# A bilinear matmul kernel: row tiles loaded and transposed three at a time, one product of the first triple moved to the front, and the opening loads put in another order

## The chip, the cores and the metric

The kernel runs on one core of a Trainium2 chip. A core has five engines that run side by side: TensorE (PE, with its weight loads shown as PEld), VectorE (DVE), ScalarE (ACT), GpSimd (POOL) and SyncE (SP). DMAs are issued from the queues of SP, ACT and POOL. The metric is device microseconds of one execution; lower is better.

## The reference

```python
"x":  (16, 512, 1024) float32,  "w1", "w2": (1024, 768) float32

def reference(x, w1, w2):
    y1 = np.matmul(x, w1)
    y2 = np.matmul(x, w2)
    return (np.tanh(y1) * y2).astype(np.float32)
```

## The kernel before, in words

The 8192 rows of x are 64 row tiles of 128 rows (`MT`). Both weights together have 1536 columns, which the kernel takes as three blocks of 512: `a` (the first 512 columns of w1), `g` (the last 256 of w1 and of w2 together) and `b` (the first 512 of w2). The inner dimension of 1024 is cut into two halves of four 128-row slices (`KH` = 4). All operands of the matmuls are float16.

The first four row tiles (`HEAD`) are multiplied plainly: 8 matmuls for each block, in the order a, g, b, while the weights are still arriving (`plain`, `mm`, L421 of the kernel before). The other 60 tiles form 20 triples. A triple's 18 block products (3 row tiles x 2 halves x 3 blocks) are replaced by 15 products p0 to p14 of four matmuls each (`product`, L444). Their left operands are a row tile's transposed half or a sum of such halves (`A_SUMS`, made on VectorE at L412, named S10, S3, S15 and so on); the right operands are weight blocks or sums of blocks (`B_SUMS`, made once on VectorE at L403, written B24, B26 and so on). Between the products, results are copied out of PSUM on ScalarE (copies and seeds, L448) and added on VectorE (L454); `C_OPS` lists these steps with what each needs. Names such as p7.0 mean product p7 of triple 0. Outputs are a tanh on ScalarE (L457) and a multiplication on VectorE (L462): m0, m1 and m2 for the three 512-column parts of a triple, mh0 to mh2 for the 256-column parts. In the first four triples m0 to m2 are done as two halves of 256 columns (`HALVED`).

**Who decides the order.** `Planner` is a list scheduler that runs when the kernel is built. Each step is an `op` with a cost, a due time, what it needs, and for DMAs a time at which it should land (`lands`, `LANDING`). The order that it finds for each engine is then pinned; on the chip each engine works in that order, with semaphore waits. TensorE's order of products is written by hand: `PE_ORDER` for a triple in general, `FIRST_ORDER` for triple 0, `LAST_ORDER` for the last. An entry with a plus belongs to the triple before.

**Loads of the start.** ACT's queue loads a0 to a3. SP's queue loads the halves of the first four row tiles (x00 is half 0 of tile 0), a4 to a7 and the g slices, as float32 into the `arena` or into `early_x` (`on_sp`, L338, L345, L348). VectorE and ScalarE cast them to float16 (L359 on VectorE, L357 on ScalarE). POOL's queue loads the b slices and whole row tiles, cast by the DMA itself (L350, L353): first a `gate` that reads the cast slice g0 (L484), then the eight b slices, then row tiles 6, 4, 5, then tiles 7, 8, 9. Tiles 0 to 6 are transposed on TensorE (`transpose_pe`, L371: four 128x128 transposes for a half tile, named PT60 for half 0 of tile 6) and evacuated (e60).

**Loads and transposes later.** Tiles 7 to 63 are transposed by a DMA on SP's queue (T7 to T63, L378), out of 8 float16 buffers (`xh`) into 12 transposed ones (`xt`). From tile 10 on, a load (L10 and so on) on POOL's queue stands behind a hold: POOL copies one column of the transpose of four tiles earlier (`AHEAD` = 4, `hold_loads`, L481), so POOL stops until that transpose has landed, and then issues one load. SP's queue also carries the output stores (L418). ScalarE sums the absolute values of every tile (L381, D7 and so on), for a check at the end.

**Set aside already.** For tiles 0 to 2 the b product is copied out of its bank by ScalarE (yb0, L431) and multiplied much later on VectorE (L435).

Of the kernel before, what the change touches and what calls it, by code (L numbers as in the profile page):

```python
# [226 lines left out]
def kernel(  # L227
# [68 lines left out]
    def xh_place(mt):  # L296
        return (mt - HEAD) % XH_BUFS

    def xh_before(mt):
        return next((m for m in range(mt - 1, 1, -1) if xh_place(m) == xh_place(mt)), None)  # L300

# [18 lines left out]
    def xh(mt):  # L320
        return xh_bufs[xh_place(mt)]
# [11 lines left out]
    def fill(e, chain):  # L333
        for cols in FILL:
            constants(bank(chain), cols)

    def load_first(e, mt, h):
        pin(nc.sync.dma_start(x_first[mt][:, half(h)], xf[mt][:, half(h)]))  # L338

    def cast_x(e, mt, h):  # L340
        copy(e, xh(mt)[:, half(h)], x_first[mt][:, half(h)])

# [8 lines left out]

    def load_x(e, mt):
        pin(nc.gpsimd.dma_start(xh(mt), xf[mt]))  # L353

# [82 lines left out]
    def place(i, name):  # L437
        if name[0] == "c":
            return bank((i, name))
        return c_bufs[name, i % C_BUFS]  # L440

    def product(e, i, dst, a, b, begins):
        for k in range(KH):
            pin(nc.tensor.matmul(place(i, dst), x_operand(i, a)[:, k, :], w_rhs(b, k),  # L444
                                 start=begins and k == 0, stop=k == KH - 1, skip_group_check=True))
# [36 lines left out]

    def gate(e, s, k):
        pin(nc.gpsimd.tensor_copy(held, w_cols(s, k)[:, :1]))  # L484

# [3 lines left out]
    FINE = (5, 36, 37, 45)  # L489
    START = 28.6  # L490
    ORIGIN = START - 6 * SLOT

# [16 lines left out]
    rows_in = (HEAD + 2, HEAD, HEAD + 1)  # L509
    GATE = ("g", 0)  # L510
    in_order = on_sp[4:] + late + [f"x{mt}" for mt in rows_in]
# [3 lines left out]
    for n in in_order:  # L515
        now += 1.25 if n in in_order[-3:] else size[n[0]]
        lands[n] = now + (LAG if now > LAG_FROM else 0.0)
# [3 lines left out]
    for n, what in enumerate(on_sp):  # L521
        before = [f"L{on_sp[n - 1]}"] if n else []
        if what[0] == "x":
            op(f"L{what}", {"sp": 0.05}, 0.1 * n - 100, [], load_first, int(what[1]), int(what[2]), issued=before, lands=lands[what])
        else:
            s, k = what[0], int(what[1])
            j = slices.index((s, k))
            old = [slices[i - SLOTS] for i in range(j, j + 1 + (s == "g")) if i >= SLOTS]
            op(f"L{what}", {"sp": 0.05}, 0.1 * n - 100, [], load_w, s, k, int(what[2]) if s == "g" else None, issued=before,
               behind=[f"c{a}{b}" for a, b in old], lands=lands[what])  # L530
    op("gate", {"pool": 0.1}, 0.0, ["c%s%d" % GATE], gate, *GATE)
    for n, what in enumerate(late):
        op(f"c{what}", {"pool": 0.58}, 0.1 * n, [], load_w, "b", int(what[1]), issued=[f"c{late[n - 1]}" if n else "gate"], lands=lands[what])
    for n, mt in enumerate(rows_in):
        op(f"L{mt}", {"pool": 0.58}, 1 + 0.1 * n, [], load_x, mt, issued=[f"L{rows_in[n - 1]}" if n else f"c{late[-1]}"],
           behind=[f"cx{m}{h}" for m in range(2, HEAD) for h in range(2) if xh_place(m) == xh_place(mt)], lands=lands[f"x{mt}"])
# [7 lines left out]
    all_casts = [f"c{s}{k}" for s, k in slices if s != "b"]  # L544
    for t in range(2):
# [12 lines left out]
    for mt in range(HEAD):  # L558
# [4 lines left out]
        op(f"D{mt}", {"act": 1.05}, START + 8, [f"Lx{mt}0", f"Lx{mt}1"], abs_x, mt, hold=11 + 4 * mt)  # L563
    for mt in rows_in:
        for h in range(2):
            by_pe(mt, h, lands[f"x{mt}"] - 2, f"L{mt}")

# [16 lines left out]
    def reuse_out(mt):  # L584
        return [f"st{mt - O_BUFS}"] if mt >= HEAD + O_BUFS else []

# [80 lines left out]
    for i in range(TRIPLES):  # L667
# [10 lines left out]
        for o in C_OPS:  # L678
# [10 lines left out]
            if kind in ("seed", "copy", "add"):  # L689
                before = []  # L690
                if o[3][0] == "s":
                    before = [f"{r}.{i - C_BUFS}" for r in readers[o[3]]] if i >= C_BUFS else all_casts
                if kind == "add":
# [7 lines left out]
            if kind in ("t", "th"):  # L701
                lo, n = (0, F) if kind == "t" else (F, G)
                op(f"{name}.{i}", {"act": 0.5 if n == F else 0.285}, due, needs, c_tanh, i, r, o[4], lo, n, o[5],
                   behind=reuse_out(mt) + ([f"{FIRST_READER[name]}.{i}"] if i == TRIPLES - 1 and name in FIRST_READER else []), chains=chains)
            elif kind == "m" and i < HALVED:
                for t in range(2):
# [6 lines left out]
    for mt in range(MT):  # L713
        i = (mt - HEAD) // 3 if mt >= HEAD else -1
        if mt < HEAD:
            kept = mt == HEAD - 1
            for t in range(2 if mt < 2 else 0):
                op(f"st{mt}{'ag'[t]}", {"sp": 0.05}, 1e3, outs[mt][t:t + 1], store, mt, t * F, (F, G)[t], behind=[f"p12.{11 + 2 * mt}"], xfer=0.5)
            if mt >= 2:
# [9 lines left out]
        else:  # L729
            op(f"st{mt}", {"sp": 0.05}, slot_of[max(i, 0), "p2"] + 12, outs[mt], store, mt, behind=late, xfer=1.0)  # L730
    for mt in range(BY_PE, MT):
        back = xh_before(mt)
        free = [] if back is None else ([f"PT{back}0", f"PT{back}1"] if back < BY_PE else [f"T{back}"]) + ([f"D{back}"] if back >= HEAD else [])
        before = f"L{mt - 1}" if mt > BY_PE else f"L{rows_in[-1]}"
# [4 lines left out]
        op(f"T{mt}", {"sp": 0.05}, None, [f"L{mt}"], transpose, mt, issued=[f"T{mt - 1}"] if mt > BY_PE else [],  # L739
           behind=xt_readers[mt - XT_BUFS] if mt >= XT_BUFS and mt - XT_BUFS != HEAD - 1 else [], xfer=1.2, latency=LANDING.get(mt, 1.0 if mt < HEAD + 6 else 3.0))  # L740
    for mt in range(HEAD, MT):
        i, r = divmod(mt - HEAD, 3)
        soon = START + 6 + 1.1 * r if i == 0 else slot_of[i, "p7"] + (2, 0, -4, -8)[min(i, 4) - 1] + 4.3 * r
        op(f"D{mt}", {"act": 1.05}, soon + 4, [f"L{mt}"], abs_x, mt, hold=soon)

# [123 lines left out]
```

## Time and profile before

| | |
|---|---|
| median of 3 runs | 297.87 us (297.68 to 299.07) |
| profiled execution: its own time | 297.88 us |
| profiled execution: span in the profile | 296.3 us |
| mean granted TensorE clock | 0.997 |
| PE, DVE, ACT, POOL busy | 289.6, 257.4, 226.3, 49.2 us |
| DMA traffic | 63.51 MB, mean 214 GB/s |

The span is what the profile covers; the device time adds what lies around it, 1.6 us here. "Idle before" in a row is the engine's idle time just ahead of those instructions, with what ended it. A matmul's start is recorded, its end is modelled, so that the records of successive matmuls overlap.

### The profile page before, as it was taken

Reading aid. Unit: us, or ns where it says so; the run is one execution under the profiler, and the core shown is the slowest. Engines: PE = TensorE matmul, PEld = TensorE weight load, DVE = VectorE, ACT = ScalarE, POOL = GpSimd, SP = SyncE. Lnnn points to the kernel's source line nnn. Section 1 sums busy time; section 2 is a strip of 40 time slices with the busy share of each in tenths; the row PEclk is TensorE's granted clock in tenths of the full one; section 3 lists DMA queues with packets and bytes.
Section 4 is the critical chain, followed back from the end, with each engine's and each line's share of the span. In section 5 each row is a group of like instructions: output and inputs, shape, how many; then the busy total and the mean of one; then the engine's idle time right before and its main releaser. Section 6 shows DMA issues by size and latency. Waiting matters only on the chain. (4 is left out here: it accounts for less than half of the span.)

```text
span 296.3 us, 4677 instructions
## 1 busy us (share of the span) xinstructions
PE 289.6 (98%) x1374; PEld 131.9 (45%) x1374; DVE 257.4 (87%) x552; ACT 226.3 (76%) x453; POOL 49.2 (17%) x129
## 2 busy tenths in 40 slices
PE   7999999999999999999999999999999999999994
PEld 3344444444444444444444444444444444444442
DVE  1679899989999998888989898898989989898785
ACT  3586899699978979797797988768686776868442
POOL 0063033020213021102110120031012110000000
PEclk9999999999999999999999999999999999999998
DMA  6999999999999999999999999999999999340334
GB/s 215 388 307 204 183 160 149 229 197 237 224 253 271 215 198 252 237 144 253 233 234 162 221 191 218 195 310 223 221 235 232 261 269 298 127 162 25 136 141 164
DMA packets 84715, 63.51 MB, mean 214 GB/s; under 512 B 62800, under 2 KB 66896, under 8 KB 84688
## 3 DMA queue, kind: packets, MB, share of 16 engines
q1 hardware_dynamic: 73888, 44.84, 62.9%
q0 software_dynamic: 9792, 16.78, 37.2%
q10 hardware_dynamic: 1008, 1.57, 1.5%
q8 instruction: 11, 0.18, 0.3%
q14 instruction: 16, 0.13, 0.2%
HBM read 39.85 MB, written 25.17 MB: 219 GB/s over the span
## 5 line engine op out<-in xcount | busy, mean ns | idle before, releaser
L444 PE MATMUL bank<-b,early_x 128*128 128x512 f16 x640 | 148.3, 379 | 0.1
L444 PEld LDWEIGHTS <-early_x 128*128 128x128 f16 x800 | 78.1, 98 | 95.0 <-issue 0.7
L454 DVE TENSOR_TENSOR bank<-bank,arena 128x512 f32<-128x512 f32 x100 | 69.6, 697 | 14.4 <-ACT arena L448 8.8
L448 ACT ACTIVATE arena<-bank 128x512 f32<-128x512 f32 x100 | 59.4, 596 | 28.7 <-PE bank L444 28.5
L462 DVE TENSOR_TENSOR o<-o,bank 128x256 f32<-128x256 f32 (+1 forms) x132 | 64.3, 512 | 6.1 <-ACT o L457 5.4
L381 ACT ACTIVATE junk<-xh 128x1024 f16<-128x1024 f16 x60 | 63.3, 1054 | 0.2
L444 PEld LDWEIGHTS <-xT 128*128 128x128 f16 x400 | 39.0, 98 | 46.6 <-issue 0.3
L444 PE MATMUL bank<-b,xT 128*128 128x512 f16 x240 | 58.3, 379 | 0.0
L457 ACT ACTIVATE o<-bank 128x256 f32<-128x256 f32 (+1 forms) x80 | 34.5, 436 | 16.0 <-DVE bank L454 11.7
L444 PE MATMUL bank<-wh,xT 128*128 128x512 f16 x160 | 41.1, 379 | 0.0
L444 PE MATMUL bank<-wh,early_x 128*128 128x512 f16 x160 | 40.9, 379 | 0.0
L481 POOL CAST held<-xT 128x1 f32<-128x1 f16 x54 | 12.3, 227 | 159.4 <-DMA xT<-xh 159.3
L353 POOL DMA_DIRECT2D xh<-in_x_dram x60 | 31.9, 532 | 17.2 <-issue 7.7
L412 DVE TENSOR_TENSOR early_x<-early_x,xT 128x512 f16<-128x512 f16 x80 | 33.2, 419 | 0.5
L448 ACT ACTIVATE bank<-bank 128x512 f32<-128x512 f32 x40 | 21.5, 574 | 7.3 <-DVE bank L454 6.2
L457 ACT ACTIVATE o<-arena 128x512 f32<-128x512 f32 x40 | 25.1, 628 | 1.2 <-DVE arena L454 1.2
L421 PE MATMUL bank<-wh,xT 128*128 128x512 f16 x72 | 18.5, 379 | 0.5 <-DVE wh L359 0.3
L412 DVE TENSOR_TENSOR early_x<-xT,xT 128x512 f16<-128x512 f16 x40 | 16.8, 419 | 0.0
L412 DVE TENSOR_TENSOR early_x<-xT,early_x 128x512 f16<-128x512 f16 x40 | 16.8, 419 | 0.0
L454 DVE TENSOR_TENSOR bank<-arena,bank 128x512 f32<-128x512 f32 x20 | 13.9, 695 | 2.4 <-ACT o L457 0.9
L454 DVE TENSOR_TENSOR arena<-bank,arena 128x512 f32<-128x512 f32 x20 | 13.7, 683 | 0.2
L454 DVE TENSOR_TENSOR arena<-arena,bank 128x512 f32<-128x512 f32 x20 | 13.6, 681 | 0.0
(47 smaller groups left out, 134.7 us busy)
## 6 DMA issues: line engine op xcount, KB each, us to landing
out_dram<-o SPq DMA_DIRECT2D x58, 384.0 KB, 5.3
xh<-in_x_dram POOLq DMA_DIRECT2D x60, 256.0 KB, 6.8
arena<-in_w_dram SPq DMA_DIRECT2D x12, 256.0 KB, 5.6
early_x<-in_x_dram SPq DMA_DIRECT2D x8, 256.0 KB, 5.0
arena<-in_w_dram ACTq DMA_DIRECT2D x4, 256.0 KB, 5.9
wh<-in_w_dram POOLq DMA_DIRECT2D x8, 128.0 KB, 5.1
out_dram<-o SPq DMA_DIRECT2D x4, 256.0 KB, 6.5
xT<-xh SPq DMA_TRANSPOSE x57, 6.9
```

The source lines that it names most:

```text
L353: pin(nc.gpsimd.dma_start(xh(mt), xf[mt]))
L381: pin(nc.scalar.activation(junk[:, :src.shape[-1]], src, ACT.Abs, scale=scale, accum_out=sums[:, column:column + 1]))
L412: pin(engine[e].tensor_tensor(x_operand(i, v), x_operand(i, a), x_operand(i, b), OP[how]))
L421: pin(nc.tensor.matmul(bank(chain)[:, :rhs.shape[-1]], xt(mt)[:, k, :], rhs, start=first, stop=k == KO - 1, skip_group_check=True))
L444: pin(nc.tensor.matmul(place(i, dst), x_operand(i, a)[:, k, :], w_rhs(b, k), start=begins and k == 0, stop=k == KH - 1, skip_group_check=T ...
L448: pin(nc.scalar.activation(place(i, dst), place(i, src), ACT.Copy, scale=float(sign)))
L454: pin(nc.vector.tensor_tensor(place(i, dst), a, b, ALU.add if signs == (1, 1) else ALU.subtract))
L457: pin(nc.scalar.activation(out_tile(HEAD + 3 * i + r)[:, lo:lo + n], place(i, src)[:, :n], ACT.Tanh, scale=float(sign)))
L462: pin(nc.vector.tensor_tensor(o, o, place(i, src)[:, at:at + n], ALU.mult))
L481: pin(nc.gpsimd.tensor_copy(held, xt(mt)[:, 0, :1]))
```

## The change

It has five parts.

1. **p7.0 early.** p7 of triple 0 leaves the fixed sequence of products and is planned at 13.0 us, among the plain a products. It needs the first half of row tile 6, which SP's queue now loads as float32 (x60, behind x01 and ahead of x11) into a free part of the arena, and VectorE casts. The slots of the arena change places (s376 behind s64), and a slot's first use waits only for the casts of what was staged in it, so that the copy of p7.0 can be written early.
2. **FIRST_ORDER** of triple 0 becomes 10 6 1 12 9 11 14 8.
3. **POOL's loads of the start** are mixed: b0, b4, b1, b5, the second half of tile 6, tile 4, b2, the two halves of tile 5, b6, b3, b7. Row tile 5's and 6's halves are transfers of their own.
4. **Batches of a triple.** From tile 10 on there is one hold for three loads, on the second transpose of the triple before. Within a triple the loads go in the order second, first, third. The tiles of the first triple are taken in the order 6, 4, 5, those of the second 7, 9, 8. Landing times for the planner are written out for tiles 7 to 15.
5. **m0.0 and m2.0 set aside.** Both banks are copied on ScalarE into out tiles of triple 2 that are not yet in use (of tiles 11 and 10), and the multiplications are done whole on VectorE, not before 55 and 54 us. Row tile 0 is stored in one DMA instead of two.

The numbers of matmuls, transposes, row loads' bytes and stores' bytes are unchanged. The core of the diff (helpers that only rename or pass on an argument are left out):

```diff
-FIRST_ORDER = "7 10 1 6 12 9 11 14 8"
+FIRST_ORDER = "10 6 1 12 9 11 14 8"
...
-    AHEAD, FREE = 4, 3
-    LANDING = {HEAD + 6: 5.8, HEAD + 7: 4.1, HEAD + 8: 3.9}
+    FREE = 3
+    TURNS = (2, 0, 1), (0, 2, 1)
+    LANDING = {7: 35.9, 9: 37.2, 8: 38.4, 10: 44.9, 11: 46.1, 12: 47.3, 13: 53.8, 14: 55.0, 15: 56.2}
+    rows = list(range(HEAD)) + [HEAD + 3 * i + r for i in range(TRIPLES) for r in (TURNS[i] if i < len(TURNS) else (0, 1, 2))]
+    turn = {mt: n for n, mt in enumerate(rows)}
...
+    ASIDE = {"m0": (HEAD + 7, 55.0), "m2": (HEAD + 6, 54.0)}
...
+    S_NAMES.insert(1, S_NAMES.pop(0))
...
+    STAGED = SLOTS - 2
...
+    def slot_casts(name):
+        n = S_NAMES.index(name) * C_BUFS
+        return [f"c{s}{k}" for j, (s, k) in enumerate(slices) if s != "b" and n <= j % SLOTS < n + C_BUFS] + [f"cx{HEAD + 2}0"] * (n <= STAGED < n + C_BUFS)
...
+    def c_aside(e, r, src, borrowed):
+        pin(nc.scalar.copy(out_tile(borrowed)[:, :F], place(0, src)))
+
+    def aside_mul(e, r, borrowed):
+        o = out_tile(HEAD + r)[:, :F]
+        pin(nc.vector.tensor_tensor(o, o, out_tile(borrowed)[:, :F], ALU.mult))
...
+    P7 = 13.0
...
+    position["p7", 0] = 0
...
-    plan.strict = [f"{p}.{i}" for _, i, p in sequence]
+    plan.strict = [f"{p}.{i}" for _, i, p in sequence if (p, i) != ("p7", 0)]
+    slot_of[0, "p7"] = P7
...
-    on_sp = "x00 x10 x20 x30 x01 x11 a4 a5 x21 a6 x31 a7".split() + [f"g{k}{t}" for k in range(KH) for t in range(2)]
-    late = [f"b{k}" for s, k in slices if s == "b"]
-    rows_in = (HEAD + 2, HEAD, HEAD + 1)
+    on_sp = "x00 x10 x20 x30 x01 x60 x11 a4 a5 x21 a6 x31 a7".split() + [f"g{k}{t}" for k in range(KH) for t in range(2)]
+    by_pool = "b0 b4 b1 b5 x61 x4 b2 x51 x50 b6 b3 b7".split()
+    GATES = {"b0": ("cg0", w_cols("g", 0)[:, :1])}
...
-    for mt in range(BY_PE, MT):
+    loads = rows[BY_PE:BY_PE + FREE] + [rows[n + r] for n in range(BY_PE + FREE, MT, 3) for r in (1, 0, 2)]
+    for n, mt in enumerate(loads):
...
-        if mt >= BY_PE + FREE:
-            op(f"H{mt}", {"pool": 0.1}, None, [f"T{max(mt - AHEAD, BY_PE)}"], hold_loads, max(mt - AHEAD, BY_PE), issued=[before])
+        if n >= FREE and n % 3 == 0:
+            held_by = rows[BY_PE + n - 2]
+            op(f"H{mt}", {"pool": 0.1}, None, [f"T{held_by}"], hold_loads, held_by, issued=[before])
```

More of the change, by code (lines that the diff above doesn't have):

```diff
@@ L296, in xh_place @@
     def xh_place(mt):
-        return (mt - HEAD) % XH_BUFS
+        return (turn[mt] - HEAD) % XH_BUFS
     def xh_before(mt):
-        return next((m for m in range(mt - 1, 1, -1) if xh_place(m) == xh_place(mt)), None)
+        return next((m for m in rows[turn[mt] - 1:1:-1] if xh_place(m) == xh_place(mt)), None)
     pin = tc.keep_in_program_order
@@ L335, in fill, with x_staged @@
             constants(bank(chain), cols)
+    def x_staged(mt, h):
+        return x_first[mt][:, half(h)] if mt < HEAD else arena[:, STAGED * F:(STAGED + 1) * F]
     def load_first(e, mt, h):
-        pin(nc.sync.dma_start(x_first[mt][:, half(h)], xf[mt][:, half(h)]))
+        pin(nc.sync.dma_start(x_staged(mt, h), xf[mt][:, half(h)]))
     def cast_x(e, mt, h):
-        copy(e, xh(mt)[:, half(h)], x_first[mt][:, half(h)])
+        copy(e, xh(mt)[:, half(h)], x_staged(mt, h))
     def load_w(e, s, k, t=None):
@@ L350, in load_w, with load_x @@
             pin(nc.gpsimd.dma_start(w_cols(s, k), wr[1][:, k, :F]))
-    def load_x(e, mt):
-        pin(nc.gpsimd.dma_start(xh(mt), xf[mt]))
+    def load_x(e, mt, cols=slice(0, K)):
+        pin(nc.gpsimd.dma_start(xh(mt)[:, cols], xf[mt][:, cols]))
     def copy(e, dst, src):
@@ L481, in hold_loads, with gate @@
         pin(nc.gpsimd.tensor_copy(held, xt(mt)[:, 0, :1]))
-    def gate(e, s, k):
-        pin(nc.gpsimd.tensor_copy(held, w_cols(s, k)[:, :1]))
+    def gate(e, src):
+        pin(nc.gpsimd.tensor_copy(held, src))
     MM = 0.2158
@@ L514 @@
     now = 9.2
-    for n in in_order:
-        now += 1.25 if n in in_order[-3:] else size[n[0]]
+    for n in arrivals:
+        now += 1.25 if n in by_pool and n[0] == "x" and len(n) == 2 else size[n[0]]
         lands[n] = now + (LAG if now > LAG_FROM else 0.0)
@@ L527 @@
             j = slices.index((s, k))
-            old = [slices[i - SLOTS] for i in range(j, j + 1 + (s == "g")) if i >= SLOTS]
+            js = range(j, j + 1 + (s == "g"))
+            old = [f"c{a}{b}" for a, b in (slices[i - SLOTS] for i in js if i >= SLOTS)] + [f"cx{HEAD + 2}0"] * (STAGED in js)
             op(f"L{what}", {"sp": 0.05}, 0.1 * n - 100, [], load_w, s, k, int(what[2]) if s == "g" else None, issued=before,
[L530 to L536, printed above, removed]
+               behind=old, lands=lands[what])
+    op(f"cx{HEAD + 2}0", {"dve": 0.37}, lands["x60"] - 1, ["Lx60"], cast_x, HEAD + 2, 0,
+       behind=[f"cx{m}{h}" for m in range(2, HEAD) for h in range(2) if xh_place(m) == xh_place(HEAD + 2)])
+    issued, x_loads = [], {(HEAD + 2, 0): (f"cx{HEAD + 2}0", lands["x60"])}
+    for n, what in enumerate(by_pool):
+        if what in GATES:
+            after, src = GATES[what]
+            op(f"gate{what}", {"pool": 0.1}, 0.1 * n, [after], gate, src, issued=issued)
+            issued = [f"gate{what}"]
+        if what[0] == "b":
+            name = f"c{what}"
+            op(name, {"pool": 0.58}, 0.1 * n, [], load_w, "b", int(what[1]), issued=issued, lands=lands[what])
+        else:
+            mt, h = int(what[1]), what[2:]
+            free = [f"cx{m}{k}" for m in range(2, HEAD) for k in range(2) if xh_place(m) == xh_place(mt)]
+            name = f"L{mt}{'abc'[int(h)] if h else ''}"
+            op(name, {"pool": 0.58}, 0.1 * n, [], load_x, mt, half(int(h)) if h else slice(0, K), issued=issued, behind=free, lands=lands[what])
+            for k in range(2):
+                if h in ("", str(k)):
+                    x_loads[mt, k] = name, lands[what]
+        issued = [name]
+    last_early = name
     landed = {}
@@ L543 @@
             op(f"c{s}{k}", CAST.get(f"{s}{k}", CAST[s]), landed[s, k] + 0.3, [f"L{n}" for n in loads], cast_w, s, k)
-    all_casts = [f"c{s}{k}" for s, k in slices if s != "b"]
     for t in range(2):
@@ L563 @@
         op(f"D{mt}", {"act": 1.05}, START + 8, [f"Lx{mt}0", f"Lx{mt}1"], abs_x, mt, hold=11 + 4 * mt)
-    for mt in rows_in:
+    for mt in rows[HEAD:BY_PE]:
         for h in range(2):
-            by_pe(mt, h, lands[f"x{mt}"] - 2, f"L{mt}")
+            by_pe(mt, h, x_loads[mt, h][1] - 2 - 0.1 * h * (mt == HEAD + 1), x_loads[mt, h][0])
     def made(mt):
@@ L584, in reuse_out @@
     def reuse_out(mt):
-        return [f"st{mt - O_BUFS}"] if mt >= HEAD + O_BUFS else []
+        aside = [f"{name}.0" for name, (borrowed, _) in ASIDE.items() if mt == borrowed]
+        return aside + [f"st{mt - O_BUFS}"] if mt >= HEAD + O_BUFS else []
     def finals(mt, s, due, last):
@@ L691 @@
                 if o[3][0] == "s":
-                    before = [f"{r}.{i - C_BUFS}" for r in readers[o[3]]] if i >= C_BUFS else all_casts
+                    before = [f"{r}.{i - C_BUFS}" for r in readers[o[3]]] if i >= C_BUFS else slot_casts(o[3])
                 if kind == "add":
@@ L704 @@
                    behind=reuse_out(mt) + ([f"{FIRST_READER[name]}.{i}"] if i == TRIPLES - 1 and name in FIRST_READER else []), chains=chains)
+            elif i == 0 and name in ASIDE:
+                borrowed, at = ASIDE[name]
+                op(f"y{name}.0", {"act": 0.5}, due + 1, [n for n in needs if n[0] != "t"], c_aside, r, o[4], borrowed, chains=chains)
+                op(f"{name}.0", {"dve": 0.6}, at + 6, [f"y{name}.0"] + [n for n in needs if n[0] == "t"], aside_mul, r, borrowed, hold=at)
+                outs[mt].insert(0, f"{name}.0")
             elif kind == "m" and i < HALVED:
```

19 lines of the change are left out of this document (10 added, 9 removed).

## The prediction

> **What bounds the kernel now.** I read the page first, then TensorE's timeline, because a busy share of a pipelined engine hides short gaps.
>
> ```profile
> PE 289.6 (98%) x1374; PEld 131.9 (45%) x1374; DVE 257.4 (87%) x552; ACT 226.3 (76%) x453; POOL 49.2 (17%) x129
> ...
> L444 PE MATMUL bank<-b,early_x 128*128 128x512 f16 x640 | 148.3, 379 | 0.1
> ```
>
> TensorE is busy in 98% of the span, and the largest group of product matmuls had 0.1 us of idle time ahead of its 640 instructions: once the triples run, nothing makes it wait. But a matmul's end is modelled (379 ns each), so I count from start to start in the timeline (columns: start, duration, engine and line, tiles, how many):
>
> ```profile
> 12.37 1.03 PE L421 MATMUL bank<-wh,xT 128*128 128x512 f16 x4
> 13.52 0.40 PE L371 MATMUL bank<-ident_h,xh 128*128 128x128 f16 x4
> 14.19 1.02 PE L421 MATMUL bank<-wh,xT 128*128 128x512 f16 x4 [0.27 <-DVE wh L359]
> 15.05 0.39 PE L371 MATMUL bank<-ident_h,xh 128*128 128x128 f16 x4
> 15.27 1.11 PE L421 MATMUL bank<-wh,xT 128*128 128x512 f16 x4
> 16.22 1.03 PE L421 MATMUL bank<-wh,xT_kept 128*128 128x512 f16 x4
> 17.15 1.24 PE L421 MATMUL bank<-wh,xT 128*128 128x512 f16 x5
> ...
> 24.09 4.91 PE L421 MATMUL bank<-wh,xT 128*128 128x512 f16 x22
> 28.84 0.61 PE L371 MATMUL bank<-ident_h,xh 128*128 128x128 f16 x8
> 29.29 0.59 PE L421 MATMUL bank<-wh,xT 128*128 128x512 f16 x2
> ...
> 32.34 4.92 PE L444 MATMUL bank<-b,early_x 128*128 128x512 f16 x20
> 37.13 1.02 PE L444 MATMUL bank<-wh,early_x 128*128 128x512 f16 x4
> ```
>
> From 24.09 to 28.84 are 22 matmuls: 0.216 us each, so a product of four is 0.864. From 28.84 to 29.29 two half tiles are transposed: 0.22 each. What is over is lost time. While the a slices arrive: 13.52 - 12.37 - 0.864 = 0.29; 14.19 - 13.52 - 0.22 = 0.45; 0.09 ahead of 16.22; 0.07 ahead of 17.15; together 0.90. In the first triple: 37.13 - 32.34 - 20 x 0.216 = 0.47. These 1.37 us are all that the change can win in the stretch that it rearranges; the order of the last triple isn't touched. The sum below is made against 297.88, the profiled execution's own time, of which 1.6 lie outside its span of 296.3; the median of the three runs is 297.87. Of that, 1.37 is 0.46%, and about 0.5%, 1.5 us, is what a measurement of this kernel can tell from no change.
>
> **The change part by part.** *p7 of triple 0 among the a products.* p7.0 (0.864, today behind the transposes of 28.84) and the transpose of its half tile (0.22, one of that block) move to about 12.7. The half tile x60 is now loaded on SP's queue ahead of x11, a4 and all that follows. What one more piece costs there is told by VectorE's casts, each of which waited for a landing:
>
> ```profile
> 10.73 0.43 DVE L359 CAST xh<-early_x 128x512 f16<-128x512 f32 x1 [0.18 <-DMA early_x<-in_x_dram]
> 11.41 0.43 DVE L359 CAST wh<-arena 128x512 f16<-128x512 f32 x1 [0.25 <-DMA arena<-in_w_dram]
> 12.08 0.43 DVE L359 CAST wh<-arena 128x512 f16<-128x512 f32 x1 [0.24 <-DMA arena<-in_w_dram]
> ```
>
> These are x11, a4 and a5: a piece every 0.68. x60 takes x11's place at 10.73, so that with cast, transpose and evacuation p7.0 can start near 12.5. All behind it lands 0.68 later: TensorE reaches the first g product at 17.15 + 0.68 = 17.83, but with 0.864 + 0.22 = 1.08 of later work done. Won: 1.08 - 0.68 = 0.40. The lower end is -0.28, if x60 itself comes a piece late and p7.0, fixed in its place, holds up what stands behind it; the upper is the whole 0.90. I take 0.40, the queue being paced by its data in row after row. The added cast of 0.43 lies in VectorE's waits between these casts, 0.18 to 0.25 each, and so delays one of them by some 0.2 before the next landing absorbs it; without them each cast behind would be 0.43 late.
>
> *First triple, and the b slices mixed with row tiles.* The products of triple 0 now begin with p10, half tiles are transposed between b products, and b6, b3, b7 come last. From the first g product to the first that needs b7 TensorE has 57 matmuls and five half tiles: 57 x 0.216 + 5 x 0.22 = 13.4, so it gets there at 31.2. When does b7 land? Today's POOL queue stops once for a landing, ahead of the third row tile, and two queries of single issues give the landings of the eighth slice and of that tile:
>
> ```profile
> 24.03 1.06 POOL L353 DMA_DIRECT2D xh<-in_x_dram  x2 [1.05 <-DMA wh<-in_w_dram]
> ```
>
> ```profile
> L350 POOL DMA_DIRECT2D wh<-in_w_dram x1: 587/587/587, 21.3 to 21.3; - x1
> ...
> DMA to landing us min/median/max: 5.5/5.5/5.5
> ```
>
> ```profile
> L353 POOL DMA_DIRECT2D xh<-in_x_dram x1: 535/535/535, 24.0 to 24.0; - x1
> ...
> DMA to landing us min/median/max: 6.6/6.6/6.6
> ```
>
> The slice lands at 26.8 and three tiles later it is 30.6: 1.27 a tile. The change takes half a tile out of POOL's queue and puts it into SP's, so b7, now behind all of them, lands at about 30.7: 0.5 ahead of TensorE. VectorE then makes two sums for p12:
>
> ```profile
> 29.89 1.29 DVE L403 TENSOR_TENSOR b<-b,b 128x1024 f16<-128x1024 f16 x2
> ```
>
> With 1.3 for them and 0.4 for a row sum between, p12's operand is there at 32.4, and TensorE, with p6 and p1 (1.73) and b7's first product ahead of it, comes at 33.2. Row tiles in earlier mean that the sums behind the lost 0.47 start earlier too. I take 0.30 of it. Ends: +0.47, and -0.8 if b7 comes a tile later (31.97 against 31.2).
>
> The Trainium skill, "DMA: Bandwidth & Descriptors", section "Anatomy of one DMA — SWDGE (gpsimd) path", speaks against cutting tiles up: it fits about 2.0 us as fixed cost of each DMA. Paid in line, POOL's one additional transfer would put b7 at 32.7 and this sum 1.5 higher. The rows disagree: whole tiles follow each other at 1.27, so no fixed 2.0 is paid in line.
>
> *m0.0 and m2.0 set aside.* Four half-bank multiplications leave VectorE between 42 and 45 us, two whole-bank ones come back after 55, and ScalarE gets two copies out of banks. A piece of ScalarE's timeline, and two windows (behind the span: TensorE, weight loads, VectorE, ScalarE):
>
> ```profile
> 42.09 0.60 ACT L457 ACTIVATE o<-bank 128x512 f32<-128x512 f32 x1 [0.15 <-DVE bank L454]
> 42.58 1.05 ACT L381 ACTIVATE junk<-xh 128x1024 f16<-128x1024 f16 x1
> ```
>
> ```profile
> 40.00:50.00 10.00, 10.00 (x48) 4.54 (x47) 9.97 (x24) 9.76 (x20) 2.31 (x5) 1.00 1.20 177
> 50.00:60.00 10.00, 10.00 (x48) 4.43 (x46) 9.95 (x26) 7.24 (x15) 1.58 (x6) 1.00 1.10 205
> ```
>
> VectorE, full from 40 to 50 (9.97), gets room. ScalarE takes on 2 x 0.60 with 0.24 free, which pushes an Abs sum into the next window, where 2.76 are free; without that cover a copy or seed stands behind an Abs sum and TensorE waits up to 1.05, once. TensorE waits for neither engine there today, so there is nothing to win: 0, with that lower end.
>
> *Loads and transposes by triples.* POOL's holds fall from 54 to 18, and each lets three loads go. Of the DMA in the window from 38 to 44 us:
>
> ```profile
> q0 software_dynamic: 525, 0.98, 98.0%
> q1 hardware_dynamic: 8, 0.00, 0.2%
> ...
> xT<-xh SPq DMA_TRANSPOSE x2, 6.5
> ```
>
> Two transposes (q1) were issued in it, and none moved data while the row loads (q0) ran: the memory side works in turns. So a round counts, from hold to hold in POOL's timeline; the slowest of the early ones:
>
> ```profile
> 59.95 0.18 POOL L481 CAST held<-xT 128x1 f32<-128x1 f16 x1 [5.61 <-DMA xT<-xh]
> ...
> 74.09 0.19 POOL L481 CAST held<-xT 128x1 f32<-128x1 f16 x1 [4.57 <-DMA xT<-xh]
> ```
>
> 14.1 us for four tiles with their stores (these are the holds that read the transposes four tiles apart): 3.5 a tile, so 10.6 for three. TensorE's triple lasts 15 x 0.864 = 12.96, and the batch gains on it. Cost 0. Its start is VectorE's first sum of triple 1:
>
> ```profile
> 36.28 0.43 DVE L412 TENSOR_TENSOR early_x<-xT 128x512 f16<-128x512 f16 x1 [0.63 <-DMA xT<-xh]
> ```
>
> The bytes ahead of T7 are the same, so it lands near 36.3 as today, and VectorE again idles there while TensorE, fed by sums already made, doesn't. Stores on SP now stand behind three transposes at a time; the next writer of their out tile is three triples off, which covers it.
>
> Sum: 297.88 - 0.40 - 0.30 = 297.2 us.
>
> **The rivals.** *Nothing is won*: the idle time only moves, because TensorE is bound by landings until 17 us and b7's margin of 0.5 is used up: 297.9. Against it: 1.08 of work leaves a stretch without idle time. *b7 late*: POOL's queue, with one transfer more, stops again as at 24.03 and b7 comes a tile later: 0.8 paid, the 0.30 not won, 298.3. The page's fixed 2.0 would make it 298.7 by the same mechanism. *T7 late*: VectorE works in order, and behind its first sum of triple 1 stand the adds of triple 0. Up to about 0.5 is covered; from there each microsecond is one of TensorE, so that T7 two tiles (2.5) late gives 297.2 + 2.0 = 299.2, and 2.9 late 299.6. For it: three transposes are now issued together; against: the same three stand first in SP's queue today. *The round, slower than before*: held on a transpose of its predecessor, a triple's round takes longer than TensorE's 12.96. That is the point from which it decides. If three tiles took 13.5, nearly as long as four do today, TensorE would lose 0.54 in each of some 16 triples, less a lead of about 3 from the start: +5.8, 303. The turns seen above speak against it, since a turn of three loads is shorter than one of four. *Faster by over 1.5*: the whole 1.37 and something else besides; nothing shows that.
>
> **How the numbers follow.** The forecast has 0.50, nothing won 0.22, b7 late 0.10, T7 late 0.08 (half of it past 1.5 us), the round 0.07, faster by over 0.5% 0.03. Slower by over 0.5%: 0.04 + 0.07, and 0.05 for two of the smaller delays together, taken from the first three: 0.16. Within 0.5%: the remaining 0.81. The range goes from 296.6, nearly all of the 1.37 won, to 299.6, T7 2.9 late; it leaves out the round and the far ends.
>
> **What would show it.** Right: the first g product near 17.8; triple 0 from p6 on without lost time over 0.1; p14.0, today at 37.13, near 36.3, and the distance kept to the end; holds 9 to 12 apart until buffers, not transposes, pace them. Wrong: TensorE waiting for a wh landing near 31, VectorE idle over 1 us at a sum that reads xT, or lost time that returns once in a triple. A time under 296.4 would mean idle time that I haven't seen.

## The result, and the profile after

The changed kernel takes 311.6 us (median of 6 runs, 310.09 to 313.01) against 297.81 for the kernel before (6 runs): the ratio is 1.0453, 95% interval 1.0417 to 1.0489. It is slower by 13.8 us; the forecast was 297.2. The profiled execution took 310.09 us, 308.5 of them in the span. Some executions of any kernel here are disturbed and some per cent longer; the times below leave them out, and from the profiles of e6 and e10, which are of such executions, only the places of waits are read.

The opening went as forecast. TensorE's timeline after:

```profile
12.85 1.03 PE L457 MATMUL bank<-wh,xT 128*128 128x512 f16 x4
...
17.63 1.24 PE L430 MATMUL bank<-wh,xT 128*128 128x512 f16 x5
...
31.34 2.75 PE L457 MATMUL bank<-b,early_x 128*128 128x512 f16 x12
33.93 0.59 PE L430 MATMUL bank<-wh,xT 128*128 128x512 f16 x2
34.36 1.89 PE L457 MATMUL bank<-b,early_x 128*128 128x512 f16 x8
36.12 1.02 PE L457 MATMUL bank<-wh,early_x 128*128 128x512 f16 x4
```

p7.0 runs at 12.85, the first g product starts at 17.63, and from p6 at 31.34 to p14 at 36.12 there are 22 matmuls in 4.78 us, 0.217 each: no lost time. p14.0 is 1.01 us earlier than before (37.13).

What was lost is in the page's groups. Behind the busy times come TensorE and VectorE, then ScalarE's tanhs that read a sum in the arena and write a row tile's output (two in a triple, t2 for its third row tile and t1 for its second), then POOL's holds:

```profile
PE 292.6 (95%) x1374; PEld 131.8 (43%) x1374; DVE 254.3 (82%) x552; ACT 222.5 (72%) x454; POOL 42.3 (14%) x94
...
L457 PE MATMUL bank<-b,early_x 128*128 128x512 f16 x640 | 149.0, 379 | 6.7 <-ACT arena L461 6.7
...
L467 DVE TENSOR_TENSOR bank<-bank,arena 128x512 f32<-128x512 f32 x100 | 69.3, 693 | 30.2 <-ACT arena L461 29.2
...
L470 ACT ACTIVATE o<-arena 128x512 f32<-128x512 f32 x40 | 24.6, 626 | 23.5 <-DMA out_dram<-o 19.4
...
L501 POOL CAST held<-xT 128x1 f32<-128x1 f16 x18 | 4.5, 249 | 196.4 <-DMA xT<-xh 196.4
```

and t2 in the kernel before:

```profile
L457 ACT ACTIVATE o<-arena 128x512 f32<-128x512 f32 x40 | 25.1, 628 | 1.2 <-DVE arena L454 1.2
```

Read from the right: ahead of these tanhs ScalarE stood idle 23.5 us instead of 1.2, and 19.4 of them ended with an *output store* (DMA out_dram<-o). An out tile is used again nine row tiles later, so t2 of triple 10 writes where row tile 27, of triple 7, still lay. Behind t2, in ScalarE's order, stand the copies and seeds; VectorE waits 29.2 us for these, TensorE 6.7 and more. One such stall, in the timeline of all engines (SP's rows are issues):

```profile
150.38 0.83 SPq L427 DMA_DIRECT2D out_dram<-o  x1
...
158.11 2.64 SPq L387 DMA_TRANSPOSE xT<-xh  x2
...
160.85 0.53 SPq L427 DMA_DIRECT2D out_dram<-o  x1
161.47 1.30 SPq L387 DMA_TRANSPOSE xT<-xh  x1
...
163.73 1.15 ACT L470 ACTIVATE o<-arena 128x512 f32<-128x512 f32 x2 [1.94 <-DMA out_dram<-o]
164.78 1.06 ACT L461 ACTIVATE bank<-bank 128x512 f32<-128x512 f32 x2
165.41 1.02 PE L457 MATMUL bank<-wh,early_x 128*128 128x512 f16 x4 [0.81 <-ACT bank L461]
```

From 151.2 to 158.11 SP's queue stands still: its head is the transpose of row tile 37, whose load hasn't landed. Behind two transposes stands the store of row tile 27, issued at 160.85. t2 starts at 163.73, having waited 1.94, then the seeds, and TensorE has waited 0.81. From triple 10 to triple 18 each of the nine t2 starts 0.08 us behind the landing of such a store; counted by these landings the waits are 21.1 us (the page puts 1.7 of them down to VectorE).

How long SP's queue stood at a transpose whose load hadn't landed (total, times, longest), after and before:

```profile
SPq L387 <- DMA xh<-in_x_dram: 141.8, 19, 15.8
```

```profile
SPq L378 <- DMA xh<-in_x_dram: 71.0, 28, 16.0
```

The store's place in SP's order is not what is new. In the kernel before the first store of triple 7 also stands behind transposes of triple 11, but it is issued at 148.41, and the t2 that needs it runs at 161.27. There the transposes are early: from triple 5 on a triple's first transpose lands 8.5 to 18.9 us ahead of the first row sum that reads it. I call that distance the lead; after the change it is 0.5 to 3.0 us in triples 3 to 10.

Why is the load late? POOL's timeline and, for the same round (the way from one hold to the next), SP's:

```profile
176.16 0.18 POOL L501 CAST held<-xT 128x1 f32<-128x1 f16 x1 [11.26 <-DMA xT<-xh]
176.70 1.59 POOL L362 DMA_DIRECT2D xh<-in_x_dram  x3 [0.35 <-issue]
190.28 0.18 POOL L501 CAST held<-xT 128x1 f32<-128x1 f16 x1 [11.99 <-DMA xT<-xh]
```

```profile
183.79 4.89 SPq L387 DMA_TRANSPOSE xT<-xh  x3
```

A round is a chain in which no second batch of loads is under way: 0.54 from hold to loads, 7.09 until the first transpose can be issued, 6.49 until the second has landed and the next hold runs. This round takes 14.1 us, while TensorE's triple takes 12.95.

### The profile page after: what moved, and what is told of

Same layout as the page of the kernel before. It is cut to its first block, busy times and chain, and to the rows that moved or that the text cites. A ratio compares the mean times of both kernels' runs of the same rounds, so it can differ in the third digit from the quotient of the medians.

```text
span 308.5 us, 4589 instructions
## 1 busy us (share of the span) xinstructions
PE 292.6 (95%) x1374; PEld 131.8 (43%) x1374; DVE 254.3 (82%) x552; ACT 222.5 (72%) x454; POOL 42.3 (14%) x94
## 5 line engine op out<-in xcount | busy, mean ns | idle before, releaser
L467 DVE TENSOR_TENSOR bank<-bank,arena 128x512 f32<-128x512 f32 x100 | 69.3, 693 | 30.2 <-ACT arena L461 29.2
L461 ACT ACTIVATE arena<-bank 128x512 f32<-128x512 f32 x100 | 57.7, 596 | 12.8 <-PE bank L457 12.8
L475 DVE TENSOR_TENSOR o<-o,bank 128x256 f32<-128x256 f32 (+1 forms) x128 | 62.1, 512 | 5.4 <-ACT o L470 4.4
L457 PEld LDWEIGHTS <-xT 128*128 128x128 f16 x400 | 38.3, 98 | 50.1 <-issue 5.6
L470 ACT ACTIVATE o<-bank 128x256 f32<-128x256 f32 (+1 forms) x80 | 33.5, 438 | 27.4 <-DVE bank L467 26.5
L457 PE MATMUL bank<-wh,xT 128*128 128x512 f16 x160 | 41.0, 378 | 1.2 <-ACT o L470 1.1
L470 ACT ACTIVATE o<-arena 128x512 f32<-128x512 f32 x40 | 24.6, 626 | 23.5 <-DMA out_dram<-o 19.4
L501 POOL CAST held<-xT 128x1 f32<-128x1 f16 x18 | 4.5, 249 | 196.4 <-DMA xT<-xh 196.4
L430 PE MATMUL bank<-wh,xT 128*128 128x512 f16 x72 | 19.5, 379 | 0.1
L467 DVE TENSOR_TENSOR bank<-arena,bank 128x512 f32<-128x512 f32 x20 | 13.8, 688 | 0.3 <-PE bank L457 0.3
L390 ACT ACTIVATE junk<-wh 128x768 f16<-128x768 f16 x16 | 13.6, 848 | 0.0
```

The source lines that it names most:

```text
L390: pin(nc.scalar.activation(junk[:, :src.shape[-1]], src, ACT.Abs, scale=scale, accum_out=sums[:, column:column + 1]))
L430: pin(nc.tensor.matmul(bank(chain)[:, :rhs.shape[-1]], xt(mt)[:, k, :], rhs, start=first, stop=k == KO - 1, skip_group_check=True))
L461: pin(nc.scalar.activation(place(i, dst), place(i, src), ACT.Copy, scale=float(sign)))
L467: pin(nc.vector.tensor_tensor(place(i, dst), a, b, ALU.add if signs == (1, 1) else ALU.subtract))
L470: pin(nc.scalar.activation(out_tile(HEAD + 3 * i + r)[:, lo:lo + n], place(i, src)[:, :n], ACT.Tanh, scale=float(sign)))
L501: pin(nc.gpsimd.tensor_copy(held, xt(mt)[:, 0, :1]))
```

## The experiments

Theory A was the round itself, B the stores' place in SP's order, C another part of the change. Each kernel is the changed one with the edit shown, but for e2, which is the kernel before. "TensorE's last product" is the last row of its timeline, 291.13 before and 303.28 after; a profile shows in it what TensorE lost in that one execution. A row of the holds gives the first and the last start and their count; from these comes the mean round, 13.21 us after (18 holds from 37.1 to 261.7). The planner makes the order on SP anew for each kernel. Beside the edits shown, e1, e6 and e10 plan 3.0 us for a transpose's way, as in the kernel before (2.0 in the changed kernel and in e2), and e7, e11 and e12 have no written landing times for tiles 13 to 15.

**e1: one load for each hold, four tiles ahead, as before.**

```diff
-        if n >= FREE and n % 3 == 0:
-            held_by = rows[BY_PE + n - 2]
+        if n >= FREE:
+            held_by = rows[BY_PE + max(n - 4, 0)]
```

> The changed kernel with its batches undone alone: from row tile 10 on one hold for each load, on the transpose of four tiles earlier, loads in the order of the rows; all the rest of the change stays. Theory A, the round: a batch's hold, loads, transposes and next hold follow each other without overlap and take 13.2 us in the mean (17 rounds between the holds at 37.1 and 261.7 in the changed kernel), against 12.95 for TensorE's triple, so the transposes never get ahead and the stores queued behind them on SP come late. Then this kernel takes 296.9 to 297.6, t2 waits for stores under 1 us in total (19.4 in the changed kernel), and the transposes gain several us of lead by 150 us. Theory B, the order on SP alone: the planner's order has stores behind transposes, whatever paces the loads; SP's order is nearly the same here, so most of the loss stays: over 305. Theory C, another part of the change (the two multiplications set aside, the first triple's order, row tile 0 stored whole): 311, as changed.

Measured: 299.38 and 299.52, where theory A had 296.9 to 297.6. The row of t2, and TensorE's last product:

```profile
L470 ACT ACTIVATE o<-arena 128x512 f32<-128x512 f32 x40 | 25.0, 628 | 9.6 <-DVE arena L467 7.3
```

```profile
290.92 1.04 PE L430 MATMUL bank<-wh,xT_kept 128*128 128x256 f16 x8
```

12 of the 13.8 us go with the batches, which rules out C as the main cause, and B alone. By the stores' landings t2 waited twice, 2.3 us in total, not under 1. TensorE's last product is 0.21 earlier than before, not the 1.0 of the opening: 0.86 went to 0.25 near 77, where a transpose landed just in time for its product, and 0.61 near 124, behind a t2 that waited for a store. In both places the transposes lead by less than in the kernel before. The other 1.6 us of this time lie behind TensorE's last product; see e11.

**e2: the kernel before with the batches alone** (the same hold and order of loads as in the changed kernel).

> The kernel before with the batches alone: from row tile 10 on one hold for three loads, on the second transpose of the triple before, loads in the order second, first, third. Theories A and B: 311 to 313, with t2 waiting for stores some 20 us in total. Theory C: within 1.5 us of the kernel before, 297.8.

Measured: 306.81, ratio 1.0269 (1.0179 to 1.0360), 8.8 us of loss, not 13 to 15; by the stores' landings t2 waited for stores seven times, 16.2 us. So C falls; the batches cost 8.8 in the order of the kernel before and more in the new one. Why more isn't shown.

**e3: the hold on the first transpose of the triple before.**

```diff
-            held_by = rows[BY_PE + n - 2]
+            held_by = rows[BY_PE + n - 3]
```

> The changed kernel with each batch's hold on the first transpose of the triple before instead of the second. A transpose is issued 1.4 us behind the one ahead of it, so the round is shorter by that. Theory A: a round of 11.8 is below TensorE's 12.95; the loads get ahead until buffers pace them, and the time is 297 to 299. Theory B: stores still stand behind two or three transposes each, 305 or more. Theory C: 311.

Measured: 308.91 (305.57 to 309.52), ratio 1.0298 (1.0149 to 1.0446). ScalarE's waits (total, times, longest), and the holds:

```profile
ACT o L470 <- DMA out_dram<-o: 14.0, 4, 5.4
```

```profile
L501 POOL CAST held<-xT x18: 183/188/460, 36.0 to 250.3; 128x1 f32<-128x1 f16 x18
```

A shorter round, 12.61 us, below TensorE's 12.95; yet four waits for stores, 14.0 us. Theory A's 297 to 299 falls. The round shrank by 0.6, not by 1.4.

**e4: the stores of a triple ahead of the transposes of the triple four later, on SP.**

```diff
+        back = [f"st{rows[n - 12 + r]}" for r in range(3)] if n % 3 == 1 and n >= BY_PE + 12 else []
-        op(f"T{mt}", ..., issued=[f"T{rows[n - 1]}"] if n > BY_PE else [],
+        op(f"T{mt}", ..., issued=([f"T{rows[n - 1]}"] if n > BY_PE else []) + back,
```

> The changed kernel with SP's order changed alone: the transposes of a triple are issued behind the three stores of the triple four earlier, which in the changed kernel stand between or behind them. Theory A: t2 no longer waits for stores (under 2 us in total), but the round is still 13.2 or so, so that TensorE comes to wait for row sums: 17 rounds x 0.25 = 4.3 less 1 to 2 of lead, 300 to 301; up to 303 where the round is longer. Theory B: 297 to 298. Theory C: 311.

Measured: 303.85, ratio 1.0186 (1.0093 to 1.0279). The row of t2, the holds, and TensorE's last product:

```profile
L470 ACT ACTIVATE o<-arena 128x512 f32<-128x512 f32 x40 | 25.0, 626 | 5.4 <-DVE arena L467 5.4
```

```profile
L501 POOL CAST held<-xT x18: 183/400/1994, 37.4 to 258.2; 128x1 f32<-128x1 f16 x18
```

```profile
293.26 1.04 PE L430 MATMUL bank<-wh,xT_kept 128*128 128x256 f16 x8
```

No wait for a store is left, and 5.9 us of loss is, a little over theory A's number. The round's mean is 12.99 (13.3 without the first two, whose loads met few stores), and the lead stays at 0 to 3.4 us to the end. So theory B alone falls too. In the two profiles, each of the fastest run of its kernel, TensorE's loss splits so: from 293.26 to 303.28 are 10.0 us of stores in the way; from the 290.1 that the opening's 1.0 would have given to 293.26 are 3.1 us of the round. Another 2.1 us of that e4 run lie behind TensorE's last product (7.3 against 5.2); see e11.

The round didn't cost TensorE these 3.1 us as I expected, through row sums that wait for transposes. Two rows of e4's waits (total, times, longest):

```profile
ACT junk L390 <- DMA xh<-in_x_dram: 12.4, 10, 2.2
...
DVE early_x L421 <- DMA xT<-xh: 1.8, 6, 0.5
```

VectorE waited 1.8 us for transposes, but ScalarE 12.4 us for row loads, with Abs sums, which read the row tile before it is transposed and stand in ScalarE's order among the copies. The kernel before and e1, e3, e7 and e8 have no such wait. Once in the timeline:

```profile
109.27 1.06 ACT L390 ACTIVATE junk<-xh 128x1024 f16<-128x1024 f16 x1 [2.24 <-DMA xh<-in_x_dram]
...
111.45 0.70 DVE L467 TENSOR_TENSOR bank<-bank,arena 128x512 f32<-128x512 f32 x1 [1.84 <-ACT arena L461]
111.47 1.02 PE L457 MATMUL bank<-b,early_x 128*128 128x512 f16 x4 [0.26 <-ACT arena L461]
```

No run moves the Abs sums, so how much of the 3.1 goes this way isn't measured. I went on with theory D: both, in series.

**e9: of these stores only the one that t2 waits for goes ahead**, that of a triple's third row tile.

> As e4, but only one of the three stores is moved: the store of a triple's third row tile, whose out tile the t2 of three triples later writes, goes ahead of the transposes of the triple four later; the other two stores stay behind them. Theory D (the store that t2 waits for, and the round): t2's waits for stores go (19.4 us in the changed kernel), and what is left is the round's loss, as in e4: 302 to 305. Rival E (all stores delay the batches, or the other two stores are waited for as well): between, 306 to 310.

Measured: 300.35, ratio 1.0085 (1.0052 to 1.0118). The row of t2:

```profile
L470 ACT ACTIVATE o<-arena 128x512 f32<-128x512 f32 x40 | 25.1, 627 | 5.0 <-DVE arena L467 3.7
```

One store in three, moved by a batch, takes away 11 of the 13.8 us, so the place of the 19.4 us is shown (one wait of 1.2 is left). The time is 1.7 under theory D's range and 3.5 under e4's. In the profiles TensorE's last products are close (292.96 here, 293.26 in e4); 2.1 us of the difference lie behind them, where e4's last stores land late (see e11).

**e5: e3 and e4 together.**

> The changed kernel with both edits of e3 and e4: the hold on the first transpose of the triple before, and the stores of a triple ahead of the transposes of the triple four later in SP's order. Theory D, two causes in series: a round of 13.1 us (17 rounds between the second transposes of triples 2 and 19 in e4, 223.0 us) paces TensorE where stores don't, and stores behind late transposes pace it where they are in the way; either edit alone leaves the other. Here the round is 11.7 and no store is late: 297 to 298.5, t2 waiting for stores under 1 us in total, transposes landing over 5 us ahead of their first reader from triple 8 on. Theory A (the round alone, with the hold's place not enough because the transposes are slow under full queues): 301 to 303. Theory B (the stores alone, the rest of e4's loss being something else): 302 to 304, as e4.

Measured: 298.94, ratio 1.0020 (0.9990 to 1.0049): no measurable difference from the kernel before, and a little over theory D's 297 to 298.5. The holds, and TensorE's last product:

```profile
L501 POOL CAST held<-xT x18: 184/185/371, 36.2 to 253.7; 128x1 f32<-128x1 f16 x18
```

```profile
290.38 1.04 PE L430 MATMUL bank<-wh,xT_kept 128*128 128x256 f16 x8
```

Each edit alone left 6 to 11 us, both together leave none that the runs can tell: two causes in series. TensorE runs every triple in 12.95 and ends 0.75 ahead of the kernel before. But the round is 12.79, not 11.7, and without the first two it is 13.15, longer than TensorE's triple. The lead, 3.5 to 4.1 us in triples 3 to 6, is 0 to 2.8 from triple 7 on, where over 5 was expected. So the loop isn't faster than TensorE here; the lead from the start just lasts. Of the ten runs four took 297.4 to 297.8 and six 298.9 to 300.5 (the profiled one 299.16, with its end late as in e1).

**e7: e4 with four loads in a batch. e8: e4 with only one row of each of row tiles 4 to 60 stored.** What is a round made of?

> As e4, with four loads in a batch instead of three, held on the second transpose of the four before (loads in the order second, first, third, fourth). It tells what the round is made of. Latencies in series: a fourth tile adds only its issue and its transpose, 1.3 to 1.5, so that the round is 14.6 for four, 10.9 for three tiles, below TensorE's 12.95: the loads get ahead until the Abs sums hold their buffers, 297 to 299. Bytes, so much per tile: 13.1 x 4 / 3 = 17.5 for four, the same pace as e4, 302 to 304.

> As e4, but of each row tile from 4 to 60 only the first of its 128 rows is stored, so that the stores keep their place and their waits and lose their traffic; the output is left out but for these rows. Latencies in series: the round is 12 to 12.7 instead of 13.1, and the time 297 to 299.5. Bytes: without 384 of the 896 KB that a tile moves (load, transpose, store) the round falls under 10 us in the first triples, 297, and the transposes land over 10 us ahead by triple 8.

Measured: e7 298.81, ratio 1.0059 (0.9992 to 1.0127); e8 298.93, ratio 1.0014 (0.9992 to 1.0037). Their holds, e7 and then e8:

```profile
L501 POOL CAST held<-xT x14: 184/186/740, 37.2 to 242.9; 128x1 f32<-128x1 f16 x14
```

```profile
L504 POOL CAST held<-xT x18: 183/226/1979, 37.9 to 239.1; 128x1 f32<-128x1 f16 x18
```

Four tiles take 15.82 us, 11.9 for three; three tiles without 384 of their 896 KB take 11.84, where 13.0 x 512 / 896 = 7.4 would follow from bytes. So bytes alone don't set the round. How it splits beyond that stays open: the fourth tile cost 2.8, twice what I expected, but both means are upper bounds, since in e7 POOL also waited 8.5 us in total for Abs sums, and SP's queue, in front of stores, waited for VectorE's multiplications 50.0 us in total in e7 and 89.2 in e8. At most 2.8 a tile leaves at least 4.5 of three tiles' 13.0 to the round itself, if each tile costs the same. For three tiles the larger batch saves only about 1 us, but that is enough to pass under 12.95.

**e6: one load for each hold, and the stores ahead.**

> The changed kernel with its batches undone (as e1) and SP's order as in e4. In e1 TensorE lost 0.86 us in triples 3 to 9 to two or three waits of t2 for a store. Theory D: these go, and what the changed start won (p7.2 at 50.72 against 51.80 in the kernel before) is kept to the end: 296.8 to 297.2, where the last stores land as in the kernel before; 298.4 where they take 1.5 longer, as in e1. Theory C (another part of the change costs something too): 298 or more with TensorE's last product no earlier than in the kernel before.

Measured: 302.70 (302.28 to 304.02), ratio 1.0155 (1.0137 to 1.0174): over 5 us above theory D's 296.8 to 297.2. POOL's timeline:

```profile
139.58 0.37 POOL L501 CAST held<-xT 128x1 f32<-128x1 f16 x1 [9.61 <-DMA xT<-xh]
...
140.62 0.23 POOL L501 CAST held<-xT 128x1 f32<-128x1 f16 x1
...
141.44 0.20 POOL L501 CAST held<-xT 128x1 f32<-128x1 f16 x1
...
154.30 0.37 POOL L501 CAST held<-xT 128x1 f32<-128x1 f16 x1 [12.01 <-DMA xT<-xh]
```

Stores ahead of three transposes make these leave SP together, so three holds fall together too and the loads are a batch again. The scheme of single holds lives on stores *between* the transposes.

**e10: e1 without the two multiplications set aside** (`ASIDE = {}`).

> As e1 (one hold for each load), and m0.0 and m2.0 no longer set aside, so that row tiles 4 and 6 are stored from 50 us on and not from 57. In e1 the transposes of triples 4 to 7 landed up to 7 us later than in the kernel before, and two stores came late for t2. Theory F (the delayed stores collide with the loads that build up the lead): the lead is as in the kernel before (over 7 us at triples 5 to 9), t2 never waits for a store, and TensorE's last product starts 0.5 to 1 earlier than in the kernel before: 296.9 to 297.5, with 1.5 more where the last stores land late. Rival G (the other changes of the opening, the rows' order and the Abs sums' times, set the lead): lead and waits as in e1, 299 to 300; without the multiplications set aside TensorE may lose up to 1 us near 45.

Measured: 299.59, ratio 1.0047 (1.0026 to 1.0069), where theory F had 296.9 to 297.5 and rival G 299 to 300: F falls. TensorE's timeline:

```profile
52.07 1.02 PE L457 MATMUL bank<-wh,xT 128*128 128x512 f16 x4 [0.50 <-DVE o L475]
```

This is p7.2: without the part TensorE waits here for a VectorE multiplication, a wait that e1 hasn't. What the part is worth isn't shown, since the times of e1 and e10 don't differ by more than their runs do. What shortens the lead between 60 and 110 us in e1 stays open.

**e11 and e12: the last instruction fetch.** In e1, e5 and e7 the span ends 6.7 to 7.2 us behind TensorE's last product, before and after 5.2. The DMA view of e7 from 291.4 to the end, and that of the kernel before from 291.4:

```profile
GB/s 60 0 0 0 134 402 387 357 387 313 320 350 447 335 335 313 328 261 37 15 7 7 7 15 22 30 22 22 22 7 0 0 0 0 0 0 0 0 0 0
...
q8 instruction: 1, 0.02, 1.1%
...
out_dram<-o SPq DMA_DIRECT2D x2, 128.0 KB, 3.8
```

```profile
GB/s 351 326 359 251 25 0 0 0 0 0 0 0 100 301 401 368 418 368 318 318 334 360 318 376 310 360 334 301 134 0 0 0 0 0 0 0 0 0 0 0
...
out_dram<-o SPq DMA_DIRECT2D x2, 128.0 KB, 2.2
```

In e7 the last stores move at some 350 GB/s and then trail at 7 to 30, about a sixteenth, which is what one engine of 16 left behind would give. A 16 KB instruction fetch (q8) falls into that window in e7 and not before. All profiles that record the last landing agree: where the last fetch starts 3.2 us or more ahead of the last store's issue (before, after, e2, e9), that store lands in 2.2 us; where it starts from 0.1 ahead to 1.0 behind (e1, e3 to e7, e10), in 3.7 to 4.0.

> As e7, with one of the seven 512-column matmuls of constants at the very start replaced by sixteen of 32 columns, so that TensorE's program is some 30 instructions longer ahead of the work. In e7 and e1 an instruction fetch of 16 KB (queue q8) starts 2.4 us before the last store ends, while the last stores are being issued, and one DMA engine of the 16 finishes 1.5 us behind the others; in the kernel before it starts 6.3 us before the end. These fetches come every 250 or so of TensorE's instructions, so 30 instructions more bring the last one some 3 us forward. Theory H (the fetch delays that engine's share of the last stores): the last stores land about 2.0 us after their issue instead of 3.6 and the time is 297.0 to 297.4, faster than the kernel before by 0.5 or more. Rival: the fetch has nothing to do with it: 298.7 as e7.

> As e7, with the small matmul of the final check (8 columns, at 273.6 us) issued eleven times instead of once, which writes the same result; TensorE's program is 20 instructions longer there. In e11 the 30 instructions stood at the start and moved all fetches: the last stores landed in 2.2 us instead of 3.8, but the first fetch, now at 19.4, came upon the last g slices, which landed 1.3 us later, and TensorE lost that. Here only the last fetch moves, from 293.1 to some 291 or before, ahead of the last stores. Theory H: TensorE pays 0.4 to 0.6 for the ten matmuls and its last product starts at 291.3 to 291.6 (291.9 in the kernel before), the last stores land in about 2.1 us, and the time is 297.2 to 297.6, a little faster than the kernel before. Rival: the last stores are slow for another reason: 299.0 to 299.3.

Measured: e11 298.61, ratio 1.0027 (1.0008 to 1.0047); e12 298.85 (297.13 to 300.91), ratio 1.0042 (1.0012 to 1.0071); both above theory H's ranges. The last stores and ScalarE's last cast of g slices in e11, then the last stores in e12:

```profile
out_dram<-o SPq DMA_DIRECT2D x2, 128.0 KB, 2.2
```

```profile
22.84 1.14 ACT L366 CAST wh<-arena 128x512 f16<-128x512 f32 x2 [1.36 <-DMA arena<-in_w_dram]
```

```profile
out_dram<-o SPq DMA_DIRECT2D x2, 128.0 KB, 2.3
```

The stores' end is as theory H has it, both times: moving the fetch brings back 1.5 us. The gain isn't there: e11 lost 0.8 near 23, where the first fetch, moved as well, fell on the last g slices, and 0.7 between 70 and 92; e12's profiled run lost 0.8 near 51 and 77 and has its last product at 291.06 (291.13 in the kernel before, not the 291.9 of the expectation), and five of its eleven runs took over 299. No version here beats the kernel before: the opening's 1 us is there in the profiles, but single late transfers take back as much.

## Why the prediction was wrong

- *p7.0 early and the first triple*: right in mechanism, a little small. The g products start at 17.63 (17.83 forecast), p14.0 at 36.12 (36.3). T7 was issued at 32.1 and landed 3.6 later, at 35.7 (36.3 forecast); b7's landing, 30.9, against 30.7. (In the rival *b7 late* the fixed 2.0 gives 299.0 by the same mechanism, 1.5 paid and the 0.30 not won; 298.7 leaves the 0.30 out.)
- *m0.0 and m2.0 aside, 0*: right as a price, as far as the times of e1 and e10 tell. The reason, that TensorE waits for neither engine there, held for TensorE's old place; once TensorE is 1 us earlier, e10's profile has a wait for VectorE at p7.2 without the part.
- *Loads by triples, 0*: **the step that failed**, at two places. First, "14.1 us for four tiles ... so 10.6 for three". The holds before are one for each tile and four tiles deep: the 14.1 is the way of one tile round, with three others beside it, not the time of four in a row. Divided by four it gives a pace only because four overlap, and the change takes just that overlap away. A batch's round costs 13.0 for three (e4), not 10.6; the kernel before does three in 11.6 (54 holds from 36.4 to 241.2, 3.86 each). Second, "the next writer ... is three triples off, which covers it". The cover has to be counted in rounds on SP's queue, not in triples on TensorE: the transposes that stand ahead of the store are those of four triples later, and with a round no shorter than the triple they are issued just when t2 wants the tile. TensorE's last product shows the price of this second gap: 303.28 against 293.26 in e4, 10.0 us.
- *The rival "the round"* had the right point, a round longer than 12.96, and the wrong mechanism ("nearly as long as four do today") and size: alone it costs TensorE 3.1 us, in e4's profile. The other 10 were in no rival. The sign that I named, lost time once in a triple, came; VectorE never waited long for xT (0.7 us in total), since the store's place gave way first, and the Abs sums next (e4).
- The turns of loads and transposes, seen in one window, spoke against the rival but were beside the point: in batches a transpose lands in 3.3 us (6.9 before) and a store in 3.3 (5.3). Each transfer became faster and the loop slower.

## What to carry to other kernels

An interval between waits that overlap is no duration: before dividing it by the number of transfers, ask how many were under way, and cost a batch as a chain, its waits added up from hold to hold. Where one in-order queue carries transfers that wait for loads and stores that free buffers, price the change for the store that stands last: how long the queue's head can stand still, and who writes that buffer next. Look too for every other reader of a late load: here the check sums on ScalarE held up the copies behind them. A lead gained in an opening is kept only if every loop behind it is faster than the bounding engine.

## What the runs showed of the hardware

An instruction fetch on queue q8 is one packet of 16 KB; the last ones of these kernels took 0.9 to 1.6 us, and which transfer they fall on moves with the length of a program: with the fetch among them the last 128 KB stores took 3.8 us (e7) instead of 2.2 (e11), and the last g slices were cast 1.3 us later (e11 against e7). The Trainium skill, "DMA: Bandwidth & Descriptors", section "Why a DMA increments its semaphore by 16 and not by 1", says that a transfer is spread over up to 16 engines that finish independently and is done when the last one is. The trace agrees: 7 to 30 GB/s at the end of e7, where some 350 were moved before.
